# One gate projection as seven block products (Strassen), with the work ahead spread over the layer

## The chip, the core and the metric

One core of a Trainium2 chip runs the whole program in one launch. The metric is the device time of a run in microseconds; less is better. The core has a matrix engine (PE, with PEld for the weight loads that run beside it), a vector engine (DVE), a scalar engine (ACT), GpSimd (POOL) and SyncE (SP), whose queue issues every transfer of this kernel.

## What is computed

The reference is a trunk of two layers over 1024 tokens of width 1024. What concerns the change is this part of a layer:

```python
h = rms_norm(x, norm_w)
p = h @ w_in                                   # 9180 columns
... merge = p[..., 6108:]                      # 3 branches x 1024 columns
branches = jnp.stack([y_a * silu(dsa_z), y_b * silu(sb_z), y_c * silu(ml_z)], axis=2)
proj = jnp.einsum('bsgc,gcd->bsgd', branches, w_branch)
gates = jax.nn.sigmoid(merge.reshape(bsz, seq, 3, 1024).astype(jnp.float32))
mixed = jnp.sum(gates * proj, axis=2)
return x + (mixed @ w_out).astype(x.dtype)
```

Branch a (index 0) is a sparse attention that keeps 256 keys for each query, branch b a stick-breaking attention, branch c an mLSTM with chunks. A gate is the sigmoid of a product of `h` (1024 x 1024) and a 1024 x 1024 piece of `w_in`, one piece for each branch. The gates hang on `h` alone, so they can be computed at any time between the norm and the merge.

## The kernel before

Every product keeps float32 accuracy by splitting each operand into a high part (rounded to the matrix engine's 32-bit format) and a low rest, and summing three products (`PASSES`: high x high, high x low, low x high). `h` is kept transposed in SBUF in blocks `mov(b, k, th)`: part b, block k of 128 features, half th of the tokens (512 columns).

The function `body` writes the work of a layer as a log of instructions. They come in this order: index projections and scores for the key selection, the mLSTM (with the bisection for the 256th score, `tk_bit` and `count`, mixed in), stick-breaking attention (`sb_attn`), sparse attention (`dsa_attn`), the merge (`gate_proj`, `acc_ct`), and the output product, which is a Strassen product already (`prod`, `sums`, `cut`). A planner, `Plan.run`, then gives every engine a fixed order: it walks through its own idea of the time, and an engine that is free takes the ready instruction with the lowest key. The key is the place in the log, plus a shift where the log says so. What comes out is a static order for each engine; on the chip an engine waits wherever the next instruction of its order is not ready. Nearly all instructions carry one source line in the profile (L533 before, L544 after, the planner's `call`), since the planner issues them all.

The gates are the **work ahead** (`log.ahead`, lines 1041 to 1066). Before, all three branches are done alike, in the order 2, 1, 0: for each block d of 128 output columns the weights are loaded into `fill` buffers, cut into a high part (ACT) and a low part (POOL), and for each half of the tokens 24 matmuls of 128x512 (3 passes x 8 blocks) gather in one of two PSUM banks kept for this (`psf`). A sigmoid follows and the gate goes to DRAM (`gate_d`), from where the merge takes it back. The matmuls have their log place plus `AHEAD_SHIFT` = 7700 as key, so they fill the holes that the attentions leave on PE. Their loads, cuts, sigmoids and stores had this key:

```python
key = [pri[k] if k not in early or ops[k].eng == "PE" else self.place[k] for k in range(n)]
```

that is, the bare place in the log, which is early in the layer: they went before almost all else, as far as the 10 `fill` buffers allowed.

Of the kernel before, what the change touches and what calls it, by code (L numbers as in the profile page):

```python
# [26 lines left out]
N_FILL = 10  # L27
# [63 lines left out]
AHEAD = (2, 1, 0)  # L91
# [120 lines left out]
class Plan:  # L212
# [3 lines left out]
    def __init__(self, log, info, caps):  # L216
# [40 lines left out]
        self.early = {at[k] for k in log.early}  # L257
        self.prio = [prio[k] for k in by]
        self.place = by
        self.n = n  # L260
        for k, d in enumerate(self.deps):
            if d and max(d) > k:
                raise ValueError("the priorities do not follow the data")

    def run(self):
# [7 lines left out]
        key = [pri[k] if k not in early or ops[k].eng == "PE" else self.place[k] for k in range(n)]  # L273
# [340 lines left out]
def body(log, tiles, caps, x_in, w_in, w_uk, w_uv, kvn, conv_w, ib, fb, mln, w_br, w_out, nrm, fnrm,  # L614
# [18 lines left out]
    def fill(dt=F32):  # L633
        return tiles.new("fill", [128, 512], dt)
# [166 lines left out]
    for l in range(DEPTH):  # L801
# [239 lines left out]
        gate_d = {}  # L1041
        log.ahead, log.shift = True, AHEAD_SHIFT
        for g in AHEAD:
            for d in range(8):
                W = [[], []]
                for hb in range(2):
                    st, wh, wl_ = fill(), fill(F32R), fill(F32R)
                    SY.dma_start(st[:, :512].rearrange("p (k c) -> p k c", k=4),
                                 cols(C_MERGE + g * 1024 + d * 128, 128)[hb * 512:hb * 512 + 512, :]
                                 .rearrange("(k p) c -> p k c", p=128))  # L1050
                    S.copy(wh[:, :512], st[:, :512])
                    pool_tt(wl_, st, f(wh), ALU.subtract, 512)
                    W[0].append(wh)
                    W[1].append(wl_)
                for th in range(2):
                    p = pst("psf")
                    i = 0
                    for a, b in PASSES:
                        for k in range(8):
                            PE.matmul(p, W[a][k // 4][:, (k % 4) * 128:(k % 4) * 128 + 128], mov(b, k, th),  # L1060
                                      start=(i == 0), stop=(i == 23))
                            i += 1
                    t = fill()
                    S.activation(t[:, :512], p, AF.Sigmoid)
                    gate_d[g, d, th] = dram([128, 512])
                    SY.dma_start(gate_d[g, d, th], t[:, :512])
# [524 lines left out]
        def wm(g, ct):  # L1591
            return (None if g in AHEAD else load_w([(cols(C_MERGE + g * 1024 + ct * 256, 256), 0)]),
# [145 lines left out]
```

## Time and profile before

| | |
|---|---|
| time, median of 3 runs | 2673.18 us (2672.58 to 2675.56) |
| profiled execution | 2675.59 us, span of its instructions 2673.8 us |
| PE busy | 2641.5 us, 99% of the span, granted clock 0.999 |
| PEld, DVE, ACT, POOL busy | 2233.9, 1749.8, 1466.0, 1100.4 us |
| transfers | 243 MB, 29.5% of 16 engines' span |

The profile shows one execution, instruction by instruction. Matmuls overlap each other in the pipeline, so a busy PE of 99% does not say that it issues at its best rate; the rate is read from the number of matmuls in a stretch. Idle time is put down to the engine or transfer whose signal ended it.

### The profile page before, as it was taken

The numbers are of one execution on the slowest core, as the hardware profiler recorded it, in microseconds if no ns is written. First come the engines' busy times: TensorE is split into PE (matmuls) and PEld (weight loads), VectorE is DVE, ScalarE is ACT, GpSimd is POOL, SyncE is SP. The second block draws the span as 40 slices with busy tenths as digits, with TensorE's granted clock in tenths as the row PEclk, the third lists the DMA queues.
The fourth block names the chain that finished last, engine by engine and source line by source line (L and its number), as shares of the span: only waits on it lengthen the run. The fifth ranks groups of instructions, "written<-read, shape, count | busy, mean of one in ns | idle before, by whom it ended". The sixth has DMA issues, their size and how long they took to land.

```text
span 2673.8 us, 41885 instructions
## 1 busy us (share of the span) xinstructions
PE 2641.5 (99%) x14676; PEld 2233.9 (84%) x14676; DVE 1749.8 (65%) x4059; ACT 1466.0 (55%) x2971; POOL 1100.4 (41%) x1445
## 2 busy tenths in 40 slices
PE   8999999999999999999999999999999999999998
PEld 7888888888888888888898888888888878888886
DVE  5829789667596753426866397996666776723278
ACT  4737873545476866512445469634556577764123
POOL 4343344332342534444814253432342444433536
PEclk9999999999999999999999999999999999999999
DMA  4322232212132315564204132231111322256531
GB/s 126 90 51 68 76 79 68 64 52 69 35 94 64 89 55 185 192 222 150 69 25 121 32 103 52 68 93 51 55 57 34 98 76 79 65 173 234 176 118 71
DMA packets 252550, 245.83 MB, mean 92 GB/s; under 512 B 23514, under 2 KB 198580, under 8 KB 252340
## 3 DMA queue, kind: packets, MB, share of 16 engines
q1 hardware_dynamic: 252340, 243.16, 29.5%
q8 instruction: 116, 1.90, 0.3%
q14 instruction: 94, 0.77, 0.1%
HBM read 180.84 MB, written 62.26 MB: 91 GB/s over the span
## 4 chain that ended last, share of the span: by engine, by line
PE 90%; DVE 4%; ACT 3%; issue 2%; POOL 0%; DMA 0%; POOLq 0%; ACTq 0%; DVEq 0%
PE t L533 90%; DVE t L533 4%; ACT t L533 3%; POOL t L533 0%; ACT L533 0%; DMA t<-in_w_in_dram 0%; ACT s L533 0%; DMA t<-in_x_dram 0%; DVE s L533 0%; POOLq L1734 0%; ACTq L533 0%; DVEq L533 0%; POOLq L533 0%
## 5 line engine op out<-in xcount | busy, mean ns | idle before, releaser
L533 PE MATMUL t<-t,t 128*128 128x512 f32 (+5 forms) x13802 | 2497.4, 342 | 22.4 <-DVE t L533 10.0
L533 PEld LDWEIGHTS t<-t,t 128*128 128x128 f32 (+2 forms) x13674 | 2080.1, 183 | 384.2 <-DVE t L533 23.3
L533 POOL TENSOR_TENSOR t<-t,t 128x256 fp32r<-128x256 f32 (+5 forms) x956 | 767.9, 833 | 1006.5 <-ACT t L533 409.0
L533 DVE TENSOR_TENSOR t<-t,t 128x512 f32<-128x512 f32 (+12 forms) x1454 | 725.9, 528 | 586.1 <-ACT t L533 470.7
L533 ACT CAST t<-t 128x512 fp32r<-128x512 f32 (+6 forms) x991 | 504.0, 549 | 456.8 <-PE t L533 222.3
L533 ACT ACTIVATE t<-t 128x512 f32<-128x512 f32 (+5 forms) x697 | 343.3, 579 | 266.6 <-PE t L533 210.9
L533 ACT ACTIVATE t<-t,t 128x1024 bf16<-128x1024 f32 (+10 forms) x352 | 307.9, 887 | 61.0 <-DVE t L533 34.2
L533 ACT COPY t<-t 64x256 f32<-64x256 f32 (+4 forms) x300 | 113.0, 379 | 250.9 <-PE t L533 248.6
L533 DVE TENSOR_TENSOR_SCAN t<-t 128x256 f32<-128x256 f32 (+10 forms) x144 | 205.0, 1436 | 8.8 <-ACT t L533 8.6
L533 POOL TENSOR_SCALAR t<-t 64x512 fp32r<-64x512 f32 x128 | 83.2, 650 | 247.2 <-ACT t L533 169.4
L533 DVE SCALAR_TENSOR_TENSOR t<-t,t,t 128x512 f32<-128x512 f32 (+8 forms) x217 | 160.0, 766 | 18.0 <-ACT t L533 11.2
L533 PE MATMUL t<-s,t 128*128 128x512 f32 (+1 forms) x474 | 149.1, 385 | 0.0
L533 DVE TENSOR_SCALAR_CACHE_REDUCE t<-t,t 128x512 bf16<-128x512 f32 (+5 forms) x198 | 145.8, 763 | 1.1
L533 ACT ACT_TABLE_LOAD x105 | 134.7, 1283 | 14.0 <-PE t L533 6.6
L533 POOL TENSOR_SCALAR t<-t,t 128x128 f32<-128x128 f32 (+7 forms) x128 | 94.8, 749 | 110.4 <-DVE t L533 107.3
L533 DVE TENSOR_TENSOR s<-s,t 128x512 f32<-128x512 f32 (+1 forms) x98 | 69.3, 709 | 106.7 <-PE t L533 97.8
L533 DVE CUSTOM_DVE_ANT_0 t<-t,t 128x512 f32<-128x512 f32 (+3 forms) x160 | 92.1, 591 | 18.0 <-PE t L533 9.4
L533 PEld LDWEIGHTS t<-s,t 128*128 128x128 f32 x474 | 87.4, 188 | 19.0
L533 POOL TENSOR_TENSOR t<-s,s 128x256 fp32r<-128x256 f32 x50 | 52.5, 1075 | 44.8 <-issue 30.6
L533 DVE TENSOR_SCALAR t<-t,t 128x512 f32<-128x512 f32 (+12 forms) x94 | 52.8, 573 | 19.2 <-ACT t L533 11.0
L533 DVE TENSOR_SCALAR t<-t 128x1 f32<-128x1 f32 (+5 forms) x324 | 58.8, 190 | 5.9 <-ACT t L533 3.7
L533 DVE TENSOR_TENSOR t<-t 128x1 f32<-128x1 f32 (+6 forms) x224 | 59.0, 272 | 3.7 <-POOL t L533 1.0
(53 smaller groups left out, 811.5 us busy)
## 6 DMA issues: line engine op xcount, KB each, us to landing
t<-in_w_in_dram SPq DMA_DIRECT2D x192, 256.0 KB, 3.7
d<-t SPq DMA_DIRECT2D x134, 256.0 KB, 2.0
t<-d SPq DMA_DIRECT2D x133, 256.0 KB, 5.2
s<-d SPq DMA_DIRECT2D x103, 256.0 KB, 5.3
t<-in_w_in_dram SPq DMA_DIRECT2D x44, 512.0 KB, 5.2
d<-t SPq DMA_DIRECT2D x130, 128.0 KB, 1.8
t<-in_w_branch_dram SPq DMA_DIRECT2D x24, 512.0 KB, 6.0
t<-in_x_dram SPq DMA_DIRECT2D x16, 512.0 KB, 5.6
```

The source lines that it names most:

```text
L533: fn(*args, **kw)
```

## The change

Branches 2 and 1 (`PLAIN`) stay as they were. Branch 0's gate is computed as Strassen's seven products of 512 x 512 blocks in the Winograd form: `h` and the weights are each cut into four blocks, products 6, 5, 7 and 3 take sums of blocks. The sums of `h` (four of them, in a high and a low part) are made once in a layer and stored to DRAM (`s_d`, by `keep`); they stand at four places of the log, 1200 apart, and are no work ahead. For each of four pairs of column blocks (d, d + 4) the work ahead then runs in four sweeps with one set of sums in eight `half` buffers `ts`, which is loaded again for each sweep by `sums_of`. Products wait in DRAM between sweeps (`p_d`, `u_d`, `v_d`; sums of weights in `t1_d`, `t2_d`). Where a product goes on from a kept one, ACT copies it into the PSUM bank and the matmuls add to it, or DVE adds it afterwards (`back`). A product takes 12 matmuls of 128x512 for one column block.

The planner's key for everything of the work ahead but its matmuls is new: it is spread evenly from 500 to 7500 log places behind the end of the block. `fill` has 12 buffers where it had 10.

```diff
-N_FILL = 10
+N_FILL = 12
-AHEAD = (2, 1, 0)
+PLAIN = (2, 1)
+AHEAD = ((0,),)
+SUM_SHIFT = 1200
+LATER = 0
+SPREAD = (500, 7500)
+    def spread(self, c):
+        a, z = next((a, z) for a, z in self.blocks if a <= c < z)
+        return z + SPREAD[0] + (c - a) / (z - a) * (SPREAD[1] - SPREAD[0])
-        key = [pri[k] if k not in early or ops[k].eng == "PE" else self.place[k] for k in range(n)]
+        key = [pri[k] if k not in early or ops[k].eng == "PE" else self.spread(self.place[k]) for k in range(n)]
...
+        for k in range(4):
+            log.shift = SUM_SHIFT * (k + 1)
...
+            t = both(a21, a22, ALU.add)
+            keep(1, k, t)
+            V.tensor_tensor(t, t, a11[0], ALU.subtract)
+            pool_tt(t, t, a11[1], ALU.subtract, 512)
+            keep(0, k, t)
...
+            V.tensor_tensor(t, a12[0], t, ALU.subtract)
+            pool_tt(t, t, a12[1], ALU.add, 512)
+            keep(3, k, t)
+            keep(2, k, both(a11, a21, ALU.subtract))
...
+        def sums_of(i, ts):
+            for k in range(4):
+                for q in range(2):
+                    SY.dma_start(f(ts[k][q]), f(s_d[i][q][k]))
+            return lambda b, k: ts[k][b]
...
+            for g, d in pairs:
+                W1 = cut_w(raw(g, d, 0))
+                Z = pst("psf")
+                gprod(Z, W1, blk(0, 0))
+                t = fill()
+                S.copy(t, Z)
+                put(p_d, (g, d), t)
+                W2 = cut_w(raw(g, d, 1))
+                gprod(Z, W2, blk(0, 4), False)
+                close((g, d, 0), Z, fill())
...
+            for g, d in pairs:
+                r11, r12, r22 = raw(g, d, 0), raw(g, d + 4, 0), raw(g, d + 4, 1)
+                add(r12, r12, r11, ALU.subtract)
+                put(t1_d, (g, d), r12)
+                add(r12, r22, r12, ALU.subtract)
+                put(t2_d, (g, d), r12)
+                W6 = cut_w(r12)
+                X = pst("psf")
+                t = fill()
+                SY.dma_start(t, p_d[g, d])
+                S.copy(X, t)
+                gprod(X, W6, Sm, False)
+                S.copy(t, X)
+                put(u_d, (g, d), t)
+            Sm = sums_of(1, ts)
+            for g, d in pairs:
+                W5 = cut_w(bring(t1_d[g, d]))
+                X = pst("psf")
+                gprod(X, W5, Sm)
+                put(v_d, (g, d), back(X, u_d[g, d]))
...
```

How the order of instructions moves is seen at three places. In the rows a name is a buffer and the instruction that first writes it.

**Place 1**, PE in the second layer's sparse attention. Before, the first product of branch 0 (`t3503`) begins here, between the attention's score products (`t5509`, `t5510`, `t5528`, `t5529`); its 24 matmuls read blocks of `h` that have been in SBUF since the layer began.

```order
L533 MATMUL t3494_24861<-t3102_14848,t3490_24767 128x512
L533 MATMUL t3503_25740<-t3060_14583,t3498_25700 128x512
L533 MATMUL t5509_25747<-t5289_24670,t5473_25587 128x512
L533 MATMUL t5509_25747<-t5289_24670,t5474_25597 128x512
L533 MATMUL t5510_25755<-t5291_24675,t5473_25587 128x256
L533 MATMUL t5510_25755<-t5291_24675,t5474_25597 128x256
L533 MATMUL t3503_25740<-t3062_14589,t3498_25700 128x512
```

At the same score products the changed order has branch 0 half done: `t3842` is the last product of sweep 0, `t3848` and `t3854` the first two of sweep 1, and `s3797` and `t3803` are two of the buffers `ts`.

```order
L544 MATMUL t3842_25822<-s3797_16312,t3841_25886 128x512
L544 MATMUL t3842_25822<-s3536_17075,t3841_25886 128x512
L544 MATMUL t5844_26711<-t5643_25626,t5825_26606 128x256
L544 MATMUL t5844_26711<-t5643_25626,t5826_26617 128x256
L544 MATMUL t3842_25822<-t3801_18946,t3841_25886 128x512
L544 MATMUL t3842_25822<-t3803_20829,t3841_25886 128x512
L544 MATMUL t5857_26728<-t5641_25621,t5825_26606 128x512
L544 MATMUL t5857_26728<-t5641_25621,t5826_26617 128x512
```
```order
L544 MATMUL t5862_26753<-t5643_25626,t5825_26606 128x256
L544 MATMUL t5862_26753<-t5643_25626,t5826_26617 128x256
L544 MATMUL t3848_26759<-s3797_16312,t3846_25924 128x512
L544 MATMUL t3854_26762<-s3797_16312,t3852_25968 128x512
L544 MATMUL t5880_26769<-t5641_25621,t5825_26606 128x512
```

Four matmuls stand between the two pieces (two of 128x128, two of 128x512). So before, 16 products of 24 matmuls of the work ahead were left at this point of the second layer; now 192 matmuls are, and between the last reader of `s3797` in sweep 0 and its first reader in sweep 1 stand 13 matmuls of 4864 columns together.

**Place 2**, SP's queue at the same point, after the change (before, nothing of this stood there). The loads from `d3489` to `d3492` bring the sums of sweep 1 into buffers that sweep 0 has just read; the other transfers are stores of the attention's result, loads for its next head and, last, the store of a product of sweep 0.

```order
L544 DMA d3463_26667<-t5792_26649 128x256
L544 DMA t5925_26674<-in_w_in_dram 128x4x128
L544 DMA t3804_20839<-d3496_20767 128x512
L544 DMA t5831_26684<-d3440_16083 16x512
L544 DMA s3797_16312<-d3489_16229 128x512
L544 DMA s3536_17075<-d3490_16965 128x512
L544 DMA t3801_18946<-d3491_18760 128x512
L544 DMA t3803_20829<-d3492_20728 128x512
L544 DMA d3844_26739<-t3843_25748 128x512
```

**Place 3**, DVE in the first layer's mLSTM, where the bisection counts scores. Before, a step is three counts (`TENSOR_SCALAR` of 384, 512 and 640) and three small instructions, and the next step follows.

```order
L533 TENSOR_SCALAR t922_3515,t921_3516<-t144_1015,t916_3512 128x384
L533 TENSOR_SCALAR t923_3524,t921_3516<-t153_1035,t916_3512 128x512
L533 TENSOR_SCALAR t924_3536,t921_3516<-t162_1107,t916_3512 128x640
L533 TENSOR_TENSOR t928_3552<-t921_3516,t8_71 128x6
L533 TENSOR_SCALAR t929_3556<-t928_3552 128x6
L533 SCALAR_TENSOR_TENSOR t930_3561<-t916_3512,t929_3556 128x6
```

Now the sums of `h` (`s1258` and `s1366`, from the blocks `t47`, `t71` and their like) stand among these steps; six of 128x512 for each of the four places in a layer.

```order
L544 TENSOR_TENSOR t1183_4025<-t1176_3984,t8_71 128x6
L544 TENSOR_TENSOR s1258_3847<-s1258_3847,t47_232 128x512
L544 TENSOR_SCALAR t1184_4032<-t1183_4025 128x6
L544 TENSOR_TENSOR s1366_4022<-t47_232,t71_421 128x512
L544 SCALAR_TENSOR_TENSOR t1185_4042<-t1175_3976,t1184_4032 128x6
L544 TENSOR_TENSOR s1366_4022<-s1366_4022,t336_3950 128x512
L544 TENSOR_SCALAR s1237_4068,t1236_4069<-t144_1021,t1185_4042 128x384
```

Two of them come between a count's comparison and the next threshold, and one between that and the next count.

## Rows read from the trace of the kernel before

**Rows 1.** The page: span, and busy time of each engine.
```profile
span 2673.8 us, 41885 instructions
PE 2641.5 (99%) x14676; PEld 2233.9 (84%) x14676; DVE 1749.8 (65%) x4059; ACT 1466.0 (55%) x2971; POOL 1100.4 (41%) x1445
```
**Rows 2.** Windows: stretch, its length, each engine's busy us (count), PE clock, DMA, GB/s.
```profile
300.00:400.00 100.00, 99.68 (x504) 83.10 (x502) 82.44 (x229) 81.60 (x159) 35.98 (x49) 1.00 0.30 76
...
1200.00:1300.00 100.00, 100.00 (x433) 80.87 (x431) 68.72 (x94) 28.04 (x48) 50.04 (x59) 1.00 0.33 109
```
**Rows 3.** Windows at the end of both layers' sparse attention.
```profile
978.00:1122.00 144.00, 143.78 (x753) 118.98 (x752) 63.84 (x204) 99.51 (x176) 62.44 (x90) 1.00 0.47 152
2306.00:2448.00 142.00, 141.96 (x736) 116.64 (x735) 59.23 (x198) 92.53 (x164) 62.24 (x90) 1.00 0.44 145
```
**Rows 4.** Groups by shape, 1200 to 1300: busy us, mean ns, idle before.
```profile
L533 PE MATMUL t<-t,t 128*128 128x512 f32 x235 | 62.7, 394 | 0.0
L533 PE MATMUL t<-s,t 128*128 128x512 f32 x123 | 40.1, 394 | 0.0
L533 PE MATMUL t<-s,s 128*128 128x512 f32 x46 | 15.4, 394 | 0.0
L533 PE MATMUL t<-t,s 128*128 128x512 f32 x29 | 10.1, 394 | 0.0
```
**Rows 5.** Groups by shape over the span, of the kinds that the change adds.
```profile
L533 ACT CAST t<-t 128x512 fp32r<-128x512 f32 x359 | 209.9, 612 | 97.7 <-PE t L533 50.7 <-DVE t L533 26.1 <-DMA d<-t 10.7
...
L533 ACT COPY t<-t 128x512 f32<-128x512 f32 x48 | 27.9, 582 | 58.8 <-PE t L533 58.8
...
L533 DVE TENSOR_TENSOR t<-t,t 128x512 f32<-128x512 f32 x242 | 173.4, 721 | 243.9 <-ACT t L533 170.9 <-PE t L533 69.8 <-DMA t<-in_w_out_dram 2.1
...
L533 POOL TENSOR_TENSOR t<-t,t 128x256 fp32r<-128x256 f32 x712 | 619.1, 896 | 717.6 <-ACT t L533 390.3 <-PE t L533 196.4 <-DMA d<-t 64.0
...
L533 POOL TENSOR_TENSOR t<-t,t 128x256 f32<-128x256 f32 x56 | 39.0, 719 | 126.1 <-DVE t L533 120.2 <-DMA t<-d 5.9
```
**Rows 6.** The same view, ACT's table loads.
```profile
L533 ACT ACT_TABLE_LOAD x105 | 134.7, 1283 | 14.0 <-PE t L533 6.6 <-DVE t L533 3.4 <-issue 1.3
```
**Rows 7.** Who waited for whom: us in total, times, longest.
```profile
PEld t L533 <- DVE t L533: 23.3, 58, 3.4
PEld t L533 <- ACT t L533: 22.5, 66, 1.9
...
PEld t L533 <- POOL t L533: 13.2, 35, 1.9
...
PE t L533 <- DVE t L533: 10.0, 14, 3.3
...
PE t L533 <- ACT t L533: 4.3, 9, 1.7
...
PE t L533 <- POOL t L533: 2.0, 3, 1.5
```
**Rows 8.** Transfers, whole span: the queue, and issues with median us to landing.
```profile
q1 hardware_dynamic: 252340, 243.16, 29.5%
...
d<-t SPq DMA_DIRECT2D x134, 256.0 KB, 2.0
t<-d SPq DMA_DIRECT2D x133, 256.0 KB, 5.2
```
**Rows 9.** Issues from 2145 to 2149, then from 1169 to 1173.
```profile
t<-d SPq DMA_DIRECT2D x1, 256.0 KB, 2.7
...
t<-d SPq DMA_DIRECT2D x9, 256.0 KB, 5.6
```
**Rows 10.** DVE's timeline, 1200 to 1230: start, us, what, idle before.
```profile
1217.53 0.69 DVE L533 TENSOR_TENSOR s<-s,t 128x512 f32<-128x512 f32 x1 [2.10 <-PE t L533]
1220.31 1.86 DVE L533 TENSOR_TENSOR t<-t,t 128x512 f32<-128x512 f32 x2 [2.09 <-PE t L533]
```
**Rows 11.** POOL's timeline of the same stretch.
```profile
1220.18 5.13 POOL L533 TENSOR_TENSOR t<-t,t 128x256 fp32r<-128x256 f32 x6
```

More of the change, by code (lines that the diff above doesn't have):

```diff
@@ L257, in __init__ @@
         self.early = {at[k] for k in log.early}
+        self.blocks = [(k, next(z for z in range(k, n + 1) if z not in log.early)) for k in log.early
+                       if k - 1 not in log.early]
         self.prio = [prio[k] for k in by]
@@ L1039, in store_y @@
             SY.dma_start(f(y_d[g][1][blk][:, t0:t0 + n]), f(lo[:, :n]))
-        gate_d = {}
-        log.ahead, log.shift = True, AHEAD_SHIFT
-        for g in AHEAD:
-            for d in range(8):
[L1045 to L1054, printed above, removed]
+        s_d = [[[dram([128, 512], F32R) for _ in range(4)] for _ in range(2)] for _ in range(4)]
@@ new lines, in gprod @@
+        def gprod(p, W, B, first=True):
+            i = 0
+            for a, b in PASSES:
+                for k in range(4):
+                    PE.matmul(p, W[a][:, k * 128:k * 128 + 128], B(b, k), start=first and i == 0, stop=i == 11,
+                              skip_group_check=True)
+                    i += 1
+        def sums_of(i, ts):
+            for k in range(4):
+                for q in range(2):
+                    SY.dma_start(f(ts[k][q]), f(s_d[i][q][k]))
+            return lambda b, k: ts[k][b]
@@ new lines, in put, with close, back, bring @@
+        def put(dct, key, t):
+            dct[key] = dram([128, 512])
+            SY.dma_start(dct[key], t)
+        def close(key, src, t):
+            S.activation(t, src, AF.Sigmoid)
+            put(gate_d, key, t)
+        def back(p, kept):
+            t = fill()
+            SY.dma_start(t, kept)
+            V.tensor_tensor(t, p, t, ALU.add)
+            return t
+        def bring(kept):
+            t = fill()
+            SY.dma_start(t, kept)
+            return t
+        def blk(th, o):
+            return lambda b, k: mov(b, o + k, th)
@@ L1055, in body @@
+        for g in PLAIN:
+            for d in range(8):
+                W = [cut_w(raw(g, d, hb)) for hb in range(2)]
                 for th in range(2):
@@ L1066, in body @@
[L1066 removed]
+                    close((g, d, th), p, fill())
+        for gs in AHEAD:
+            pairs = [(g, d) for g in gs for d in range(4)]
+            for g, d in pairs:
+                W1 = cut_w(raw(g, d, 0))
+                Z = pst("psf")
+                gprod(Z, W1, blk(0, 0))
+                t = fill()
+                S.copy(t, Z)
[3 more added lines that the diff above has]
+                close((g, d, 0), Z, fill())
+            ts = [(half(F32R)[:, :512], half(F32R)[:, :512]) for _ in range(4)]
+            Sm = sums_of(0, ts)
+            for g, d in pairs:
[6 more added lines that the diff above has]
+                X = pst("psf")
+                t = fill()
+                SY.dma_start(t, p_d[g, d])
[9 more added lines that the diff above has]
+                put(v_d, (g, d), back(X, u_d[g, d]))
+            Sm = sums_of(2, ts)
+            for g, d in pairs:
+                r12, r22 = raw(g, d + 4, 0), raw(g, d + 4, 1)
+                add(r12, r22, r12, ALU.subtract)
+                W7 = cut_w(r12)
+                r21, t2 = raw(g, d, 1), bring(t2_d[g, d])
+                add(r21, r21, t2, ALU.subtract)
+                W4 = cut_w(r21)
+                Y = pst("psf")
+                gprod(Y, W7, Sm)
+                t = back(Y, v_d[g, d])
+                close((g, d + 4, 1), t, t)
+                gprod(Y, W4, blk(1, 4), False)
+                t = back(Y, u_d[g, d])
+                close((g, d, 1), t, t)
+            Sm = sums_of(3, ts)
+            for g, d in pairs:
+                W3 = cut_w(raw(g, d + 4, 1))
+                X = pst("psf")
+                t = fill()
+                SY.dma_start(t, v_d[g, d])
+                S.copy(X, t)
+                gprod(X, W3, Sm, False)
+                close((g, d + 4, 0), X, t)
```

38 lines of the change are left out of this document (33 added, 5 removed).

## The prediction, made before the run

> **What bounds the kernel now.** I read the page first: PE is busy 99% of the span, the next engine, DVE, 65% [rows 1]. That figure alone proves little, since matmuls overlap. So I looked in the windows for a stretch in which nothing can be in PE's way. From 1200 to 1300 us PE runs 433 matmuls, all of 512 columns [rows 2, 4]; 100 us / 433 = 231 ns each, 0.451 ns a column. The clock is at its full level, 2.4 GHz. There the matmul count alone sets the time. From 300 to 400, in the bisection of the mLSTM, PE is as busy, but DVE is at 82.4 us and ACT at 81.6 of the 100 [rows 2]: a stage with little room beside PE. At the end of each layer's sparse attention ACT is busy 99.5 of 144 and 92.5 of 142 us, while PE stays full [rows 3]: the work ahead fills what attention leaves. The view of waits says how much PE still loses: 75.3 us in 185 waits over PE and PEld, on DVE, ACT and POOL [rows 7], 0.41 us each; part of PEld's lie under a running matmul. So PE's work is the bound nearly everywhere, and a matmul that goes is worth its 231 ns as long as no wait takes its place.
>
> **What the change removes.** Branch 0's gate took 8 blocks x 2 halves x 24 = 384 matmuls of 128x512 in a layer. The seven products take 4 pairs x 7 x 12 = 336. So 48 go in a layer, 96 in all: 96 x 0.231 = **22.2 us of PE**. The attention's, the merge's and the other two gates' matmuls stay.
>
> **What it adds, off PE.** Counted in the code, for both layers. ACT: 88 more copies and casts of 512 columns, at 582 to 612 ns [rows 5] some 52 us; but the changed order holds 84 table loads where the trace has 105, 21 x 1.283 = 27 us less [rows 6]. Net 25 us on an engine with 1200 us free [rows 1]. DVE: 72 instructions of 128x512 at 721 ns [rows 5], 52 us. POOL: 240 of 128x256 at 719 to 896 ns [rows 5], 173 to 215 us, which takes it to about half the span. SP: 264 more transfers of 256 KB, 69 MB; at the share that 243 MB take now [rows 8] that is 8 points of the engines' time. None of the sums makes another engine the bound. Their cover is PE's own 2641 us; where the cover is thin, they cost.
>
> **Where they cost.** Three places.
>
> First, DVE and POOL beside each other. Alone a subtraction or addition of 128x512 on DVE takes 0.69 us; two that run beside POOL's run of six take 1.86 [rows 10], and those six take 0.86 each [rows 11] where the cheap kind takes 0.72 [rows 5]. The Trainium skill, GPSIMD Engine Reference, section 1 (Specifications), says that POOL shares its SBUF interfaces with DVE and contends with DVE instructions that have two SBUF inputs. The trace agrees with it by the 1.86 us. The sums of `h` are just of this kind, and 12 of DVE's 48 stand in the bisection (place 3, the third of four places in each layer), where a count waits for the one before. There DVE gets 12 x 0.72 = 9 us more, 11 if each is slowed by 1.86 / 2 - 0.69 = 0.24 us too, in some 100 us of the two layers together that DVE now fills to 82%. It fits in the 18% free. Between nothing and those 11 us I take 1, since the work ahead can fill PE meanwhile.
>
> Second, more hand-overs. In the changed order 3013 of PE's instructions wait for a signal, before it was 2854; 159 more. Of the 2854 waits 185 lasted at all in the trace, at 0.41 us each [rows 7]: 159 x 185 / 2854 x 0.41 = 4.2 us. The bounds are nothing, if the planner has room for them all, and about 28 us, if each of the 56 new products (28 in a layer) lost 0.5 us. The row of a wait on ACT (4.3 us in 9 times, 0.48 each) is the nearest to such a product; the kernel has some 9 and 14 such waits on PE in all, not hundreds, so I stay by 4.
>
> Third, the loads of a new set of sums at the three changes of sweep in each layer. A load into `ts` must wait for the last matmul that reads the old set, and PE, in order, stands at the first that reads the new. Place 1 shows 4864 columns between the two, at 0.451 ns a column 2.2 us. A load of 256 KB takes 2.7 us when it is alone and 5.6 when nine are issued together [rows 9]; the sums come eight at a time, over some 3 us, with the attention's transfers between them (place 2). The same count at the six changes gives, for the tile that is needed first, about 11, 5 and 5 us of matmuls in layer 0 and 2.2, 3 and 9 in layer 1. At 2.7 us only one change waits, 0.5 us; at 5.6 the sum is 0.6 + 0.6 + 3.4 + 2.6 = about 7. I take **4**, in the middle, since half of the eight are issued earlier than the one needed first. The Trainium skill, DMA: Bandwidth & Descriptors, section Anatomy of one DMA, gives a transfer (on the gpsimd path) about 2.0 us fixed and its bytes at 436 GB/s on top, an estimate of 2.6 us for these loads; by that the term would be 0 to 0.5 and the time 4 us less than mine. The lone load agrees with it, the group of nine does not, and the median of all, 5.2 [rows 8], is nearer to the group.
>
> **What is moved.** Before, the work ahead's own loads and cuts went first wherever there was a buffer, and 384 matmuls of branch 0 were left at place 1 of layer 1; now 192 are. So 192 x 0.231 = 44 us of filler went to earlier places. The ends of sparse attention thus have less to fill, and their ACT has fewer table loads; 99.5 and 92.5 us of ACT over 144 and 142 [rows 3] leave room for a stretch shorter by some 45 us only just. I price this at nothing as forecast, and as the second rival below.
>
> **The sum.** Profiled execution 2675.6 us (span 2673.8 and 1.8 around it): 2675.6 - 22.2 + 1 + 4 + 4 = 2662.4. The median of the runs shown is 2.4 lower, so **2660 us**, 0.5% less than before.
>
> **The rivals.**
> *No wait appears.* The planner put each reload and copy early enough, and 21 fewer table loads even shorten attention. For it speaks that before only 185 of 2854 waits lasted. Against it: place 1, where 2.2 us stand against at least 2.7. It gives 2673.2 - 22.2 = 2651, a little less with shorter waits.
> *The filler is missed.* PE was full at the ends of attention because the work ahead was there; with 44 us of it gone to earlier places, ACT's chain of scores, exponentials and copies shows. To eat the gain, 11 us in each layer must stand idle there, 8% of each stretch. For it: ACT's 99.5 of 144 [rows 3]. Against: fewer table loads, and the other places had holes to fill too, where waits would go. It gives about 2673, no change.
> *The products wait for their banks: slower.* 40 PSUM groups of branch 0 (20 in a layer) share two banks; many are filled by a load and an ACT copy, or end in a DVE addition and a store, before the bank is free. If PE reaches each of them 1 us too early, that is 40 us: 2673 - 22 + 40 = 2691. It decides from (22.2 + 5.3) / 40 = 0.7 us each. For it: the order on PE is fixed, and a load takes up to twice what it takes alone [rows 9]. Against: the waits that last now are 0.41 us [rows 7], and from place 1 on the attention's matmuls stand between products.
>
> **Chances.** Forecast (2652 to 2668) 0.60, no wait (below 2652) 0.12, filler missed (2668 to 2678) 0.17, banks (above 2678) 0.11. A change within 0.2%, 5.3 us, is about what a measurement of this kernel can't tell from none: faster 0.72, same 0.17, slower 0.11. The range runs from 2648, all saved and a little more, to 2678, where the slower rival begins.
>
> **What would show it.** In the profile after: 96 fewer matmuls, PE's busy time down by about 22 us at most, and its windows of the merge as before. The waits of PE and PEld on DVE, ACT and POOL about 4 us above 75; new waits on `t<-d` and `s<-d`, some 4 us, in the second layer's last attention; DVE's mean for 128x512 up a little. Wrong would I be if PE has idle microseconds throughout the ends of sparse attention (the filler), if waits on transfers sum to tens of us, or if the 100 us windows of the bisection hold fewer matmuls at PE's same work.

## The result and the profile after

The changed kernel takes 2693.07 us (median, 2690.29 to 2694.83), the kernel before 2674.37 beside it: a ratio of 1.0066, 95% interval 1.0053 to 1.0078. It is 19 us slower, where 2660 was forecast. The loss against the forecast is 33 us; against 2651, the rival in which no wait appears, 42.

The page of the changed kernel: span, then busy time of each engine; then two of its groups of transfers (count, size, median us to landing).

```profile
span 2690.5 us, 42740 instructions
...
PE 2635.4 (98%) x14580; PEld 2216.1 (82%) x14580; DVE 1804.2 (67%) x4131; ACT 1491.8 (55%) x3038; POOL 1284.4 (48%) x1685
...
t<-d SPq DMA_DIRECT2D x230, 256.0 KB, 4.9
d<-t SPq DMA_DIRECT2D x228, 256.0 KB, 2.3
```

The 96 matmuls are gone (14580 for 14676), and no other engine is near its limit. But PE's busy time fell by 6.1 us only [rows 1], where 22.2 us of matmuls went. A matmul of 512 columns is counted as busy for 394 ns where one starts every 231 ns [rows 2, 4], so a stand of up to some 160 ns between two of them leaves no idle time. Most of the 16 us between the two figures is such standing; up to 3 us of it may be the clock (0.998 of full speed for 0.999).

Who waited for whom on PE and PEld, the same six rows as [rows 7]:

```profile
PEld t L544 <- ACT t L544: 38.0, 100, 1.9
PEld t L544 <- DVE t L544: 35.5, 72, 3.3
...
PEld t L544 <- POOL t L544: 26.9, 49, 2.8
...
PE t L544 <- DVE t L544: 15.6, 20, 3.2
...
PE t L544 <- POOL t L544: 12.5, 16, 2.4
...
PE t L544 <- ACT t L544: 9.3, 19, 1.6
```

They sum to 137.8 us in 276 waits; before it was 75.3 in 185. Each of the six has grown. PE and PEld wait 1.9 us for loads of sums. At the ends of both layers' sparse attention alone (880 to 1150 and 2210 to 2470 us) the six sum to 66.9 us, before to 20.8: 46 of the 62 us of new waits stand there.

Windows of the changed kernel, first where the matmul count alone sets the time, then the ends of both layers' sparse attention; below them the same two ends before:

```profile
1200.00:1300.00 100.00, 100.00 (x434) 80.99 (x433) 63.74 (x88) 22.80 (x39) 50.07 (x64) 1.00 0.37 121
...
1030.00:1140.00 110.00, 102.63 (x575) 82.92 (x575) 76.50 (x243) 96.16 (x187) 63.13 (x92) 0.98 0.73 236
...
2340.00:2460.00 120.00, 113.58 (x638) 91.98 (x637) 85.25 (x272) 93.18 (x191) 78.84 (x114) 1.00 0.77 253
```
```profile
1030.00:1140.00 110.00, 108.48 (x554) 89.60 (x553) 44.86 (x129) 67.53 (x118) 45.72 (x64) 1.00 0.66 219
...
2340.00:2460.00 120.00, 120.00 (x603) 98.52 (x602) 42.17 (x134) 70.77 (x121) 47.82 (x69) 1.00 0.54 185
```

The merge runs as before, 434 matmuls in 100 us [rows 2]. At the ends of sparse attention, where PE was full [rows 3], it stands 7.4 us of 110 and 6.4 of 120 idle (before, in the same two stretches, 1.5 and 0.0), with a mean granted clock of 0.98 and 1.00. ACT is busy 96.16 of the 110 us there, before 67.53, and DVE 76.50, before 44.86. Branch 0's additions on DVE are 12 in a layer, some 9 us at 0.72 each, so most of this is attention's own work, which stands closer together than before. PE's groups by shape say the same: idle time ahead of the 128x128 matmuls, none of which is branch 0's, is 18.1 us, where it was 8.2; ahead of the 512 column ones 11.5, where it was 4.3.

```profile
L544 PE MATMUL t<-t,t 128*128 128x512 f32 x6668 | 1766.1, 403 | 11.5 <-ACT t L544 5.6 <-POOL t L544 3.8 <-DVE t L544 1.7
...
L544 PE MATMUL t<-t,t 128*128 128x128 f32 x2079 | 338.0, 272 | 18.1 <-DVE t L544 9.8 <-POOL t L544 5.3 <-ACT t L544 2.4
```

### The profile page after: what moved, and what is told of

Same layout as the page of the kernel before. It is cut to its first block, busy times and chain, and to the rows that moved or that the text cites. A ratio compares the mean times of both kernels' runs of the same rounds, so it can differ in the third digit from the quotient of the medians.

```text
span 2690.5 us, 42740 instructions
## 1 busy us (share of the span) xinstructions
PE 2635.4 (98%) x14580; PEld 2216.1 (82%) x14580; DVE 1804.2 (67%) x4131; ACT 1491.8 (55%) x3038; POOL 1284.4 (48%) x1685
## 5 line engine op out<-in xcount | busy, mean ns | idle before, releaser
L544 PE MATMUL t<-t,t 128*128 128x512 f32 (+6 forms) x13474 | 2466.7, 342 | 41.8 <-DVE t L544 15.6
L544 PEld LDWEIGHTS t<-t,t 128*128 128x128 f32 (+1 forms) x13346 | 2023.8, 183 | 405.0 <-ACT t L544 37.0
L544 POOL TENSOR_TENSOR t<-t,t 128x256 fp32r<-128x256 f32 (+4 forms) x1138 | 904.2, 825 | 909.4 <-ACT t L544 345.8
L544 DVE TENSOR_TENSOR t<-t,t 128x512 f32<-128x512 f32 (+15 forms) x1504 | 762.6, 537 | 502.6 <-ACT t L544 358.6
L544 ACT CAST t<-t 128x512 fp32r<-128x512 f32 (+4 forms) x1030 | 528.6, 551 | 480.0 <-PE t L544 214.3
L544 ACT ACTIVATE t<-t 128x512 f32<-128x512 f32 (+4 forms) x692 | 340.7, 565 | 270.8 <-PE t L544 169.0
L544 ACT ACTIVATE t<-t,t 128x896 bf16<-128x896 f32 (+11 forms) x358 | 310.9, 881 | 43.6 <-DVE t L544 24.3
L544 DVE SCALAR_TENSOR_TENSOR t<-t,t,t 128x512 f32<-128x512 f32 (+9 forms) x207 | 155.9, 781 | 25.4 <-ACT t L544 14.0
L544 DVE TENSOR_SCALAR_CACHE_REDUCE t<-t,t 128x384 bf16<-128x384 f32 (+5 forms) x198 | 145.1, 763 | 3.1 <-ACT s L544 0.9
L544 PE MATMUL t<-t,s 128*128 128x512 f32 (+1 forms) x312 | 78.2, 341 | 0.5 <-ACT t L544 0.5
```

The source lines that it names most:

```text
L544: fn(*args, **kw)
```

## The experiments

All 18 runs; each ratio is against the kernel before on the same chip. "PE's waits" is the sum of the six rows shown above (75.3 before, 137.8 after the change), where it is used below.

| run | us | ratio, 95% interval | PE's waits |
|---|---|---|---|
| spread order alone | 2673.75 | 0.9998 [0.9989, 1.0008] | |
| sums of `h` formed, not used | 2674.93 | 0.9998 [0.9989, 1.0008] | |
| block products, old order key | 2716.29 | 1.0154 [1.0139, 1.0169] | |
| block products between branches 2 and 1 | 2726.61 | 1.0191 [1.0176, 1.0206] | |
| a third bank for the work ahead | 2731.85 | 1.0207 [1.0190, 1.0224] | |
| same order, no later loads of sums | 2691.87 | 1.0063 [1.0047, 1.0080] | |
| same order, no hand-over in mid-bank | 2691.20 | 1.0060 [1.0045, 1.0075] | |
| same order, light GpSimd | 2684.14 | 1.0038 [1.0025, 1.0051] | |
| same order, no casts on ScalarE | 2683.76 | 1.0038 [1.0023, 1.0053] | |
| same order, all four of these out | 2676.80 | 1.0009 [1.0000, 1.0019] | 110.1 |
| buffers of sums taken late | 2821.59 | 1.0554 [1.0538, 1.0570] | |
| plain gates, buffers of sums held | 2676.36 | 1.0010 [1.0000, 1.0020] | |
| stripped block products, order of their own | 2683.78 | 1.0032 [1.0021, 1.0044] | |
| plain gates, 96 matmuls fewer | 2654.45 | 0.9925 [0.9908, 0.9941] | 75.5 |
| the same, weights cut twice | 2664.43 | 0.9956 [0.9941, 0.9971] | 92.0 |
| the same, short products through DRAM | 2686.16 | 1.0039 [1.0025, 1.0053] | 121.0 |
| the same, both | 2715.08 | 1.0145 [1.0130, 1.0161] | 168.0 |
| the same, short products kept in SBUF | 2656.62 | 0.9931 [0.9914, 0.9947] | 82.5 |

### The parts of the change alone

**The spread order alone**, with plain gates and the 12 buffers.

```diff
-PLAIN = (2, 1)
-AHEAD = ((0,),)
+PLAIN = (2, 1, 0)
+AHEAD = ()
...
```


> All three gates as plain products (384 matmuls each), no Strassen, no sums; only the new key (the spread) and 12 fill buffers. Theory 1 (branch 0's own instructions on ACT, POOL and DVE are late for PE, or stand in the way of the attention's): no such instructions here, so the time is that of the kernel before within 0.3%, 2666 to 2682. Theory 2 (the spread takes filler from the ends of attention, and attention's own chain shows): the loss is here too, 2690 to 2710, with some 30 us more waits in the sparse-attention stages.

2673.75: nothing lost or gained, so the new key alone does no harm to plain gates. The second rival is not tested by it: the order of this run leaves 380 matmuls of the work ahead at the score products of place 1, about as many as before (384), where the changed kernel's leaves 192. The filler has not moved here.

**The old key** with the block products.

```diff
-        key = [pri[k] if k not in early or ops[k].eng == "PE" else self.spread(self.place[k]) for k in range(n)]
+        key = [pri[k] if k not in early or ops[k].eng == "PE" else self.place[k] for k in range(n)]
```


> The changed kernel with the key of before for the work ahead (bare log place), so Strassen without the spread. Theory 1: the loss stays, 2685 to 2705. Theory 2: the filler stays at the ends of attention and the 22 us of matmuls show as gain, 2650 to 2668.

2716.29, above both ranges: the loss hangs on the block products, and the spread takes 23 us off it.

**The sums of `h` alone**: plain gates as in the first run, the sums formed and stored, read by nothing.

```diff
+        for k in range(4):
+            log.shift = SUM_SHIFT * (k + 1)
...
+            keep(2, k, both(a11, a21, ALU.subtract))
```


> All three gates plain, the new key, and the sums of h formed and stored at their four places in a layer, but not used: 48 instructions on DVE, 128 on POOL, 32 casts on ACT and 64 stores more than in the run with the spread alone (2674). If the sums are what slows the kernel: 2680 or more. The prediction's term for them and DVE beside POOL: 1 us, 2675. Theory 1: under 4 us, since the loss lies in the sparse attention and the sums are over by then.

2674.93, a ratio of 0.9998: the sums cost nothing that can be measured.

**Block products in the middle**, branch 0 between branches 2 and 1.

```diff
-        for g in PLAIN:
+        for g in PLAIN[:1]:
...
+        for g in PLAIN[1:]:
```


> The changed kernel with branch 0's products between those of branch 2 and of branch 1, so that they run in the stick-breaking attention and plain products of 24 matmuls fill the sparse attention. If the loss comes from what the sparse attention's own chain on ACT, DVE and POOL shares with branch 0 (its table loads, its products scaled on POOL): much of it goes, 2660 to 2680. If it comes from Strassen's chain wherever it runs: the waits move along, 2685 to 2700.

**A third PSUM bank** for the work ahead, so one fewer for the rest.

```diff
-N_PSF = 2
+N_PSF = 3
```


> The changed kernel with three PSUM banks for the work ahead, five for the rest (it had two and six). Theory 1a: a third bank gives PE another product to go on with while one is copied: 2670 to 2685. Theory 1b: no gain, 2690 or more, as attention has one bank less.

Both are slower than the change itself, by 34 and 39 us, the first of them above both its ranges. So neither an earlier place in the queue nor a third bank mends the loss. As both runs have a new order, and the third bank is taken from the rest, they don't show that place and banks have no part in it.

### Parts taken out, in the order of the changed kernel

Here every instruction stands at the place that it has in the changed kernel; some are left out or read other data. The planner sees the full work and makes the same order.

**Light GpSimd**: branch 0's low parts of weights are set to 0, and its sums of weights are not formed.

```diff
+        if self.tags[k] == 'block' and self.ops[k].eng == 'POOL':
+            if args[0].tensor.dtype == F32R:
+                self.pool.memset(args[0].bitcast(F32), 0.0)
+            return
```


> The changed kernel in exactly its order, but branch 0's instructions on POOL are left out or nearly: the low parts of its weights are set to zero by a memset in place of a subtraction, the sums of weights are not formed (so branch 0's gate is not the reference's). Theory 1, if POOL is the engine in the way: 8 to 20 us come back, 2673 to 2685, and the attention's waits on POOL fall. Theory 1, if it is ACT and DVE: less than 5 us come back. Theory 2: less than 3 us come back.

2684.14, 9 us back. PE's waits for GpSimd halve, from 26.9 and 12.5 us:

```profile
PEld t L551 <- POOL t L551: 13.3, 27, 1.9
...
PE t L551 <- POOL t L551: 5.8, 8, 1.5
```

**No later loads of sums**: the loads for the second to fourth sweep are left out, the products read the first set.

```diff
+        if self.tags[k] != 'reload':
+            fn(*args, **kw)
```


> The changed kernel in exactly its order, with the loads of sums for sweeps 1 to 3 left out, so that these sweeps read the sums of sweep 0 (branch 0's gate is not the reference's) and never wait for a reload. The prediction's term: 4 us come back, 2689. If the reloads were the main loss: 15 us or more, under 2678. If reloads hardly wait: within 2 us of the changed kernel's 2693.

2691.87: 1 us, inside an uncertainty of some 5 us for the difference of the two.

**No hand-over in mid-bank**: a copy in the middle of a bank reads SBUF, a prefill writes SBUF, and the second product starts its bank anew, so the kept products don't enter the gates.

```diff
+        if tag == 'mid':
+            args = [args[0], self.real(alt)]
+        elif tag == 'pre':
+            args = [args[1], args[1]]
...
+        elif tag == 'go':
+            kw = dict(kw, start=True)
```


> The changed kernel in exactly its order, with the hand-overs in the middle of a PSUM bank taken away: a copy into a bank writes an SBUF buffer instead, a copy or addition out of a bank in the middle of a pair of products reads SBUF instead, and the second product starts anew (so branch 0's gate is not the reference's). Every engine has the same number of instructions. Theory 1a (PE waits because ACT and DVE sit between two products in one bank, as the rival on banks said): most of the waits in front of branch 0's matmuls go, some 8 of 13 us, and 10 to 20 us of the time: 2673 to 2684. Theory 1b (ACT, DVE and POOL are late since they have more work, whatever the bank): less than 5 us come back, 2688 to 2693.

2691.20: 2 us. The hand-overs in the middle of a bank are not where the time is lost. The copies and additions at the end of a group stay in this run, so that part of the third rival isn't tested by it.

**No casts on ScalarE**: branch 0's products read constant weights for the high part, and the low part is `t` minus `t`.

```diff
+        if tag == 'cut' and eng == 'ACT':
+            return
+        if tag == 'cut':
+            args = [args[0], args[1], args[1], args[3]]
+        if tag[:2] == 'hi':
+            args = [args[0], self.real(alt), args[2]]
```


> The changed kernel, instructions of every engine in its order; ScalarE's cast of each weight block of branch 0 is left out (the products read constant weights in place of the cast high part, and the low part is t minus t). Theory A, the loss is ScalarE's work between a weight's landing and its product: 10 us or more come back, 2683 or less. Theory B, the loss is the order itself (short dependent pieces where long fillers stood): within 3 us of the changed kernel, 2690 to 2696. Theory C, the loss is the eight buffers that the sums hold through the layer: the same as B.

2683.76: 9 us back, just short of the 10 that theory A set.

**Matmuls only**: all four of these out at once. What stays beside the matmuls are the additions of kept products, the sigmoids, and the products' and weights' stores and loads.

```diff
+        if tag[:2] in ('hi', 'lo'):
+            args = [args[0], self.real(alt), args[2]]
+        if tag == 'add':
+            return
...
+        if tag == 'reload':
+            return
```


> The changed kernel in its order, with all that branch 0 asks of other engines between its products left out: sums of weights, ScalarE's casts, GpSimd's low parts, the hand-overs in the middle of a bank, the second to fourth loads of sums (products read constant weights). The matmuls, the additions of kept products, the sigmoids and the stores stay. Theory A: nearly all comes back and the 22 us of removed matmuls show, 2650 to 2662. Theory B: about the sum of the parts already seen (9 for GpSimd, 2 and 1) and no more, 2678 to 2685. Theory C: as B, since the buffers are held as before.

2676.80, between the ranges of theories A and B and nearer to B's: 16 us back, less than the four give one by one (21), so they overlap. The 26 us down to 2651 stay. The windows of this run:

```profile
1030.00:1140.00 110.00, 104.83 (x578) 84.55 (x578) 74.98 (x240) 89.06 (x170) 51.23 (x72) 1.00 0.75 245
...
2340.00:2460.00 120.00, 117.01 (x647) 96.41 (x646) 77.81 (x246) 82.40 (x162) 47.04 (x67) 1.00 0.75 244
```

The same stretches still stand 5.2 and 3.0 us idle, and PE's idle time ahead of the 128x128 matmuls, which are not branch 0's, is 15.6 us for 18.1 in the changed kernel and 8.2 before:

```profile
L565 PE MATMUL t<-t,t 128*128 128x128 f32 x2079 | 339.7, 273 | 15.6 <-DVE t L565 7.4 <-POOL t L565 4.8 <-ACT t L565 2.8
```

### The buffers of the sums

**Taken late**: the planner may give the eight `half` buffers only near the first product that reads them.

```diff
+                    if not forced and c == "half":
+                        return None
```


> The changed kernel, but the eight buffers of the sums are not taken until just before the first product that reads them (a planner rule; the order moves with it). Theory C: 10 to 30 us come back, 2663 to 2683. Theories A and B: within 6 us of the changed kernel, 2687 to 2699.

2821.59. It went the other way, 128 us slower, with a granted clock of 0.977: the rule makes a far worse order, and tells nothing on the theory.

**Held**: plain gates with unused sums, and the eight buffers loaded early and held till the end of the early work.

```diff
+        ts = [(half(F32R)[:, :512], half(F32R)[:, :512]) for _ in range(4)]
+        sums_of(0, ts)
...
+                SY.dma_start(held, f(ts[k][q]))
```


> The kernel with plain gates in spread order and unused sums (2674.9 before), in which eight buffers of the sums are now loaded early and held until the end of the layer's early work, and read by nothing but a store. Theory C: 10 to 30 us slower than the kernel before, 2685 to 2705. Theories A and B: within 3 us of 2675.

2676.36, some 1 to 2 us over the run without them. Theory C falls, for plain gates.

### Fewer matmuls, and an order for light work

**The stripped block products with an order of their own**: constant weights and none of the side work, known to the planner.

```diff
-                    PE.matmul(p, W[a][:, k * 128:k * 128 + 128], B(b, k), start=first and i == 0, stop=i == 11,
+                    PE.matmul(p, flat[:, :128], B(b, k), start=first and i == 0, stop=i == 11,
...
-                W1 = cut_w(raw(g, d, 0))
+                W1 = bare(raw(g, d, 0))
```


> The same stripping as in the run with matmuls only (constant weights, no sums of weights, casts, low parts, hand-overs in mid-bank or later loads of sums), but done before the planner runs, so that the order is made for the stripped work. If the 26 us that the run with matmuls only still lacked lie in an order that the planner shaped around the block products' dependences, they come back: 2650 to 2660. If they lie in there being 96 fewer matmuls to fill waits with, they stay: 2670 to 2680.

2683.78, worse than the same stripping in the order of the changed kernel, and outside both ranges. A new order brings waits of its own, so this run tells nothing apart; the next does.

**96 matmuls fewer on plain gates**: 21 of 24 in each bank of branch 0, so the last three partial products are left out there.

```diff
+                            if g or i < 21:
```


> Plain gates in the spread order (2673.75 before), with 21 matmuls of 24 in every bank of branch 0, so the same 96 matmuls fewer as with block products and nothing else changed (branch 0's last three partial products are left out). If a removed filler matmul is worth its time, 2673.75 less 22.2 is 2651.6: 2649 to 2656. If the missing matmuls leave holes in the sparse attention that nothing else fills, 2660 to 2674.

2654.45. The page of this run:

```profile
PE 2619.1 (99%) x14580; PEld 2216.7 (84%) x14580; DVE 1743.7 (66%) x4059; ACT 1474.6 (56%) x2975; POOL 1100.0 (41%) x1445
```

PE's busy time falls by 22.4 us [rows 1], the run's time by 20.3, and the waits stay at 75.5. The ends of sparse attention stay full:

```profile
1030.00:1140.00 110.00, 108.98 (x549) 89.02 (x548) 42.23 (x120) 66.14 (x114) 50.12 (x69) 1.00 0.72 247
...
2340.00:2460.00 120.00, 120.00 (x597) 98.38 (x596) 43.32 (x123) 66.39 (x111) 50.55 (x69) 1.00 0.67 232
```

So matmuls taken from the filler pay nearly in full, as long as this many stay: at the score products of place 1 this order has 334 left, the changed kernel's 192. Whether 192 are too few, the run doesn't say. The changed kernel has the very same count over the whole, 14580, and loses 39 us against this run.

### Plain gates made like block products

Here nothing depends as block products do; plain gates with 21 matmuls a bank get one property of them at a time. Each of these kernels has an order of its own.

**Weights cut twice**: branch 0's weights are loaded and cut for each half of the tokens anew, eight cuts for two blocks of columns, where block products have seven and plain gates four.

```diff
+                    if g == 0 and th:
+                        W = [cut_w(raw(g, d, hb)) for hb in range(2)]
```


> Plain gates with the 96 matmuls fewer (2654.45), and in branch 0 the weights loaded and cut for each half of the tokens anew, so eight cuts where block products have seven and plain gates four. If the doubled preparation of weights (12 buffers, ScalarE's cast, GpSimd's low part) is what loses the time, 2665 to 2685, with GpSimd's share of it near the 9 us that leaving out its low parts gave back. If not, 2652 to 2659.

2664.43, just under the first range: 10 us, a bit more than leaving out GpSimd's or ScalarE's part gave back in the changed kernel (9 each).

**Short products through DRAM**: the 21 matmuls are split into 12 and 9. The first part is copied out and stored; the second has a bank of its own, the first part is loaded and added.

```diff
+                                if not g and i == 12:
+                                    t = fill()
+                                    S.copy(t, p)
+                                    put(p_d, (g, d, th), t)
+                                    p = pst("psf")
...
+                        t = back(p, p_d[g, d, th])
+                        close((g, d, th), t, t)
```


> Plain gates with the 96 matmuls fewer (2654.45), and in branch 0 each bank's 21 matmuls split into 12 and 9 as short as block products: the first part is copied out by ScalarE and stored, the second begins a bank of its own, the kept part is loaded again and added by VectorE. If short products, each with an eviction and a trip through DRAM, are what loses the time, 2670 to 2685. If not, 2652 to 2659.

2686.16, 1 us above the first range: 32 us lost, with 32 such trips (16 in a layer), and no cut, no sum and no dependence between products beyond the pair. PE's waits and those of DVE for loads from DRAM in this run:

```profile
DVE t L544 <- DMA t<-d: 51.0, 14, 10.2
...
PEld t L544 <- DVE t L544: 34.2, 60, 3.4
...
PEld t L544 <- ACT t L544: 29.0, 90, 1.5
...
PEld t L544 <- POOL t L544: 22.1, 34, 3.2
...
PE t L544 <- DVE t L544: 19.5, 22, 3.3
...
PE t L544 <- POOL t L544: 10.1, 10, 2.7
...
PE t L544 <- ACT t L544: 6.1, 11, 1.3
```

One such place, from the timelines of PE, DVE and SP (start, length, what, idle before and its releaser):

```profile
1056.26 2.02 PE L544 MATMUL t<-t,t 128*128 128x128 f32 x12 [0.25 <-POOL t L544]
1059.72 1.38 PE L544 MATMUL t<-t,t 128*128 128x512 f32 x6 [1.44 <-DVE t L544]
```
```profile
1055.44 0.16 DVE L544 RECIPROCAL t<-t 128x1 f32<-128x1 f32 x1 [0.71 <-ACT t L544]
1058.98 4.14 DVE L544 TENSOR_TENSOR t<-t,t 128x512 f32<-128x512 f32 x9 [3.37 <-DMA t<-d]
```
```profile
1054.72 0.44 SPq L544 DMA_DIRECT2D t<-d  x1
```

The last load ahead of the addition is issued at 1054.72; DVE is done with its other work at 1055.60 and stands 3.37 us until 1058.98; PE stands 1.44 us, put down to DVE, and goes on at 1059.72, 0.74 us later, about one addition ([rows 10]: 0.69). In this place the addition of a kept product held up PE, and on DVE the eight instructions that the row has behind it.

**Both edits.**

```diff
+                    if g == 0 and th:
+                        W = [cut_w(raw(g, d, hb)) for hb in range(2)]
...
+                                    put(p_d, (g, d, th), t)
+                                    p = pst("psf")
```


> Both edits together: short products and twice the cuts, on plain gates with the 96 matmuls fewer. If the rate at which branch 0's pieces ask for buffers, banks and engines is the whole loss, 2680 to 2695, near the changed kernel's 2693. If it needs the block products' dependences (sums between sweeps, one product's result in the next's bank), 2655 to 2672.

2715.08, above both ranges and 61 us over plain gates with 96 matmuls fewer; one by one the edits cost 10 and 32. Together short pieces and more cuts cost more than the two costs added up, and more than block products lose, without any of their dependences between products.

**Short products kept in SBUF**: the split stays, ScalarE's copy and VectorE's addition too; the store and the load go.

```diff
-                                    t = fill()
-                                    S.copy(t, p)
-                                    put(p_d, (g, d, th), t)
+                                    kept = fill()
+                                    S.copy(kept, p)
...
-                        t = back(p, p_d[g, d, th])
-                        close((g, d, th), t, t)
+                        V.tensor_tensor(kept, p, kept, ALU.add)
+                        close((g, d, th), kept, kept)
```


> The run with short products on plain gates (2686.16), but the first part stays in SBUF until VectorE has added it: the store, the load and the second buffer are gone, the split into 12 and 9, ScalarE's copy and VectorE's addition stay. If the trip through DRAM (a store, a load and the time for which they hold buffers) is what costs 32 us, 2654 to 2662. If the shortness itself does it (a bank and an eviction for every 12 matmuls), 2678 to 2688. Between them, both share it.

2656.62. Of the 32 us only 2 are left; 30 were the trip, with the order that the planner makes around it. The same rows as for the run through DRAM:

```profile
PEld t L544 <- ACT t L544: 30.8, 90, 1.6
PEld t L544 <- DVE t L544: 20.5, 43, 3.3
...
PEld t L544 <- POOL t L544: 12.2, 33, 1.1
...
PE t L544 <- DVE t L544: 10.4, 12, 3.2
...
PE t L544 <- ACT t L544: 7.4, 12, 1.4
...
DVE t L544 <- DMA t<-d: 4.3, 1, 4.3
...
PE t L544 <- POOL t L544: 1.2, 3, 0.6
```

And the first layer's end of sparse attention, through DRAM and then kept:

```profile
1030.00:1140.00 110.00, 100.19 (x477) 80.83 (x476) 39.65 (x115) 58.54 (x109) 46.13 (x63) 0.95 0.64 210
```
```profile
1030.00:1140.00 110.00, 108.10 (x541) 87.73 (x540) 49.63 (x138) 76.72 (x131) 50.49 (x70) 1.00 0.70 238
```

The loss stands where most of the changed kernel's stands. Through DRAM PE gets 477 matmuls done in these 110 us, with the granted clock at 0.95 on the mean; kept in SBUF, 541 at full clock. At the second layer's end (2340 to 2460 us) the clock is 0.96 against 1.00. By these figures some 10 of the 30 us (0.05 x 110 + 0.04 x 120) are the clock's, an estimate; in the changed kernel the same figures give 2.

## Why the prediction was wrong, point by point

**PE is the bound, and a matmul that goes is worth 231 ns.** Right: 20.3 us for 96 on plain gates, where 22.2 was forecast.

**The sums of `h` on DVE and GpSimd, 1 us.** Right: no loss in the run with the sums alone. One reading behind it was not: the 0.69 us at 1217.53, called alone, was taken beside GpSimd too:

```profile
1217.39 1.44 POOL L533 TENSOR_TENSOR t<-t,t 128x256 fp32r<-128x256 f32 x2
```

Of the two instructions in 1.86 us only the second, which takes 1.07, was slowed. The change's GpSimd work did cost 9 us, but at another place than the text gave: in the low parts and sums of weights, between a weight's landing and its product, not in the bisection.

**The loads of a new set of sums, 4 us.** Probably too much: 1 us without them, where the uncertainty takes in 4, and 1.9 us of waits for them on PE and PEld. The Trainium skill, DMA: Bandwidth & Descriptors, section Anatomy of one DMA, puts a transfer on the gpsimd path at about 2.0 us and its bytes at 436 GB/s on top, an estimate of 2.6 us for these loads. From it the prediction had 0 to 0.5 for the term; the run without these loads can't tell that from 4. The loads of kept products were slower than that estimate: the median of loads of this size is 4.7 us in the run through DRAM, and single waits for them go up to 10.2 us.

**The hand-overs, 4 us: this is the step that failed.** The term was mis-sized: it took 159 more waiting instructions and let as few of them last as before, 185 of 2854 at 0.41 us. There came 91 more lasting waits and 62.5 us more in the view, three quarters of it at the ends of sparse attention, and part of it ahead of instructions that are not branch 0's (the 128x128 matmuls). Even the upper bound, 56 products by 0.5 us, gave 28. The rate of lasting waits was taken from an order in which the work ahead needed little: a load and a cut for 24 matmuls, one eviction for 24, no results to fetch. It didn't hold for the changed one. The step also left out that a block product fetches what it needs: "SP: 264 more transfers" was priced as a share of the transfer engines' time, and not as 40 stores and 56 loads of kept results in both layers together (5 and 7 for each of 8 pairs), for each of which an instruction waits or a buffer is held. How much of the new waiting comes from that is open, as said below.

**The moved filler, nothing.** Not shown. The run with the spread alone left the time unchanged, but there the filler stayed where it was (380 matmuls left at place 1).

**The rivals.** "The products wait for their banks" gave 2691, close to the 2693 measured, but as far as the runs go that is luck: without the hand-overs in mid-bank 2 us come back, not 40; only the evictions at a group's end are untested. "The filler is missed" names the right stretches, the ends of sparse attention, and PE's idle microseconds there were among the things that the text said would prove it wrong. Its time, 2673, was 20 us too low, and no run tests its mechanism.

**What is shown, and what is not.** Of the 42 us between 2693 and 2651, 16 come back with the side work (low parts, casts, mid-bank hand-overs, later loads). The other 26, or 22 against the 2654.45 measured with 96 matmuls fewer, stay open. Two causes are in view.

The first is the trip of the kept products. On plain gates 32 trips of a kept part through DRAM cost 30 us at the right place, some 10 of them by the clock, which the changed kernel doesn't lose. The changed kernel has more trips, and the run with matmuls only kept them all. That they cost the 22 to 26 us there is argued, not shown: no run of it without its trips was made. The wait through which they act on plain gates isn't seen in it, either. DVE's waits for loads are 51.0 us in the plain run; in the changed kernel the row that answers to it is 2.8 us:

```profile
DVE t L544 <- DMA t<-d: 2.8, 2, 2.1
```

so the trips there would act through the order that the planner makes around them, rather than by waits for the loads themselves.

The second is the moved filler, the prediction's second rival. The changed kernel's order, which the run with matmuls only has too, leaves 192 matmuls of the work ahead at place 1, before it was 384. The plain runs leave more: 380 (spread alone), 344 (through DRAM), 334 (96 fewer), 322 (weights cut twice) and 278 (kept in SBUF). For this cause speaks that with the side work out PE still stands 15.6 us ahead of the 128x128 matmuls, which are not branch 0's (8.2 before), and that ACT and DVE are busier at the ends than before (89.06 and 74.98 of 110 us in the first layer, before 67.53 and 44.86). The stripped products with an order of their own leave 110 and take 2683.78, but they keep their trips as well. The runs don't separate the two causes, nor either of them from the rest of the order.

No version that computes the whole reference beat the kernel before; those at 2654, 2657 and 2664 leave out three partial products of 24 in branch 0.

## What to carry to other kernels

Work that filled another chain's gaps was worth its matmul time here while it asked for little at the moment it was used (20 us for 96 plain matmuls). So price a cheaper algorithm by its pieces (matmuls per eviction, cuts per matmul, results to fetch), and not only by its matmul count and the other engines' busy shares; and look what is left to fill the last gaps. A partial result kept in SBUF cost next to nothing here (2 us for 32), the same result by way of DRAM some 0.9 us each (30 / 32, the order and the clock with it). And a time that fits a rival is no proof of it: the bank rival's sum was right, and the part of its mechanism that was tested was worth 2 us.

## What was not expected of the hardware

PE's busy time is no count of its work: after the change it fell by 6.1 us for 22.2 us fewer matmuls, on plain gates by 22.4 for the same matmuls.

Side works that cost 10 and 32 us alone cost 61 together, and four that gave back 9, 9, 2 and 1 us gave back 16: here the costs of such waits could not be added up.

Where PE stood more, its clock went down as well. In the run through DRAM it was granted 0.95 on the mean in the stretch with 100.19 us busy of 110, and 1.00 kept in SBUF, with 108.10. The changed kernel kept 0.998 over the span, 0.999 before, so at most some 3 of its 39 us are the clock's.
